# Taking the sums of squares for a norm inside the previous layer's output projection, in a two-layer streaming encoder

## The chip, the cores and the metric

One core of a Trainium2 chip runs the whole program. The metric is the device time of one execution in microseconds (us). The engines are named as the profile names them: PE does the matmuls, with PEld for its weight loads; DVE, ACT and POOL are the vector, scalar and general-purpose engines; SP only issues DMA transfers. Each engine works through its own list of instructions in order and waits at an instruction until the semaphores that it needs have come.

## The reference

Two layers run over a prompt of 2048 tokens and a sample of 64 new tokens, with a model width of 1024 and 16 heads of 64. Layer A is grouped-query attention over a sliding window, layer B attention over a band of chunks. Both have this form, in float32:

```python
def rms_norm(x, g):
    xf = x.astype(jnp.float32)
    y = xf * lax.rsqrt(jnp.mean(xf * xf, axis=-1, keepdims=True) + EPS)
    return (y * g.astype(jnp.float32)).astype(x.dtype)

def project(x, norm_g, w_in, q_g, k_g, n_heads, n_kv):
    h = rms_norm(x, norm_g)
    p = h @ w_in
    ...
    q, k, v, gate = jnp.split(p, [wq, wq + wkv, wq + 2 * wkv], axis=-1)
    ...
    return q, k, v, gate

def gated_attention_layer(...):
    qp, kp, vp, gp = project(x_p, norm_g, w_in, q_g, k_g, n_heads, n_kv)
    op = prompt_band_attention(qp, kp, vp, past_chunks, bias_fn, sinks)
    y_p = x_p + (op * jax.nn.silu(gp)) @ w_out
    ...
```

Layer B's input is layer A's output. Its norm needs one number per token: the mean of the squares of the token's 1024 values.

## The kernel before

**Data.** Activations lie in SBUF transposed, with the model's width on the 128 partitions (8 groups of 128) and the tokens along the free axis. The weights carry the norm's gain, and the per-token factor 1/rms is applied after the matmul, as the scale with which a projection leaves PSUM (`scaled`, L480, and `evacuate`, L488). So a projection may start before its tokens' factors are known; its evacuation may not. Every float32 operand of a projection is split into a high and a low part, and each product is three matmuls (L471, L472, L473; in the output projection L1269, L1270, L1271).

**Stages.** First comes layer A's input projection and attention, then layer A's output projection (668.7 to 873.8 us in the trace), then layer B's eight passes, one per pair of heads, and layer B's output projection. Between layers, x lies in HBM (`x1`). The stages overlap: projections and output projections are generators in the class `Filler` (L601), and the attention pipelines pull matmuls out of it in the gaps of their own work. The order on PE is written by hand in this way. The order on DVE, ACT, POOL and SP is set by the framework's scheduler, and some jobs go through a queue of background work (`bg`, L228).

**Layer A's output projection** (`output_jobs`, L1237) has two halves, each of 512 output columns. Each half has 8 jobs, one per block of 264 tokens (OT). A job has four groups (m = 0 to 3) of 24 matmuls, each group into one of the two PSUM buffers called pj. For every second group the residual is loaded into a tile `res` (two buffers, L1264); DVE adds the PSUM group to it (L1274), and after every second group the sum is stored to `x1` (L1276). The next job's input comes into `xraw` (tag of three buffers), ACT casts it (L376) and POOL subtracts (L377).

**Layer B's first pass** (`add_unit`, L979) takes units of 256 tokens, as two tiles of 128; the sample's 64 tokens are a unit of their own, next to last. `load_act` (L342) loads `x1` in four pieces per unit, casts (L376), subtracts (L377), and stores the split pieces for the seven later passes (L380). With `squares` set, which is so in the first pass only, each piece is also squared by ACT (L388) into a `res` tile, the two halves of that are added by DVE (L392), and the four pieces' sums are added up (L394). `token_scales` (L414) then sums over the partitions with a matmul by `ones` (L421) for each tile of tokens, adds eps on DVE (L424), and raises to the power of -0.5 on POOL (L428). It is called between the unit's first tile and its second (L1005, L1006) and puts its result into a pj buffer, the tag from which the projections' PSUM comes too. The sums over all 16 tiles of the prompt and the sample's tile are taken in nine such calls.

**Other names.** `BT` (L177) is a tile of 1920 columns that holds the attention biases; L189 loads it from `skew`. L556 makes the low part of the probabilities (`pl`), L583 is a PE transpose, L1174 and L1175 are layer B's probability-times-V matmuls, L1100 subtracts the row maximum, L306 makes the low part of weights, L917 is layer A's probability-times-V matmul, and L558 splits the cached keys and values of the sample (`KSA`, `KSB`, `VS`), which come through a `res` tile as well.

Of the kernel before, what the change touches and what calls it, by code (L numbers as in the profile page):

```python
# [11 lines left out]
AF = mybir.ActivationFunctionType  # L12
ALU = mybir.AluOpType
# [38 lines left out]
def hybrid_encoder_kernel(  # L52
# [360 lines left out]

    def token_scales(layer, unit, x, ps):  # L414
        for q, q2 in zip(x.items, x.squares):
            bg.run(q)
            bg.run(q2)
        part = x.sum[0]
        _, T, tiles = unit
        for i, (tt, t0, n) in enumerate(tiles):  # L420
            nc.tensor.matmul(ps[:, 2 * i : 2 * i + 2], part[:, i * P : (i + 1) * P], ones, start=True, stop=True)  # L421
        v = t("ms", [P, 4])
        w = len(tiles)
        nc.vector.tensor_scalar(  # L424
            v[:, : 2 * w], ps[:, : 2 * w], 1.0 / D, EPS, op0=ALU.mult, op1=ALU.add
        )
        tt = tiles[0][0]
        nc.gpsimd.tensor_tensor(  # L428
            rr[layer][:, tt : tt + w],
            v[:, : 2 * w].rearrange("p (i e) -> p i e", e=2)[:, :, 0],  # L430
            mhalf[:, :w],
            op=ALU.pow,
        )

    def row_scales(unit):
        _, T, tiles = unit
        w = len(tiles)
        tt = tiles[0][0]
        acc = t("ms", [P, 4])
        for i, (_, t0, n) in enumerate(tiles):  # L440
            r0 = (tt + i) * P
            for h in range(2):
# [6 lines left out]
                )  # L449
        v = t("ms", [P, 4])  # L450
        av = acc[:, : 2 * w].rearrange("p (i e) -> p i e", e=2)
# [195 lines left out]
    def layer_a():  # L647
# [4 lines left out]
        def add_unit(qd, place, unit):  # L652
# [58 lines left out]
            def first():  # L711
# [7 lines left out]
                for i, c in enumerate(both([project(it.tile, xc, st.w[qd], 512, o) for it, o in zip(mine, qgs)])):  # L719
                    if i == 7:  # L720
                        token_scales(0, unit, xc, psum("tp", 512, 1))
                        for it, o in zip(mine, kvs):
                            take_kv(it, o[0])
                    yield c
                for it, o in zip(mine, qgs):
                    take_qg(it, o[0])
                st.bias[0] = spread_first()
                token_scales(0, units[1], st.x[0, 1], psum("o", 512, 1))
                yield 2 * 3 * 512 / 2400
# [197 lines left out]
        def pipeline():  # L927
            N = len(items)
            for i in range(-3, N + 1):
# [5 lines left out]
                if 0 <= i < N:  # L935
                    scores(items[i])
                    bg.share(AL, AP_)
                filler.to(c0 + 0.3 * (end - c0))
# [35 lines left out]
    def layer_b():  # L974
# [4 lines left out]
        def add_unit(hp, unit):  # L979
# [7 lines left out]
            def prefetch():  # L987
                for j in range(NO):
                    assert finished["x1", j] == 2 or j * OT >= u * UT + T
                st.x[hp, u] = x = load_act(x1, u * UT, T, hp == 0, T == TS, None, xs[1], hp > 0)  # L990
                return x
# [6 lines left out]
            def gen():  # L998
# [3 lines left out]
                for e, (tt, t0, n) in enumerate(tiles):  # L1002
                    out = []
                    c = yield from project((tt, t0, n), xc, st.w[hp], 512, out)
                    if hp == 0 and e == 0:  # L1005
                        token_scales(1, unit, xc, psum("pj", 512, 2))  # L1006
                    pr = evacuate(1, tt, n, out[0], 512, P, it.gate[:, e])
                    it.prs.append(pr)
                    v, kn = pr[:n, 256:384], pr[:n, 128:256]
                    split_v(n, v, VS[:, 2] if last else VT[:, tt])  # L1010
                    it.todo += head_norm(n, pr[:n, 0:256]) + gate(n, it.gate[:n, e])
                    if last:
                        it.todo.append(store_kv(1, n, kn, v, kb_s[192:256, cols], vb_s[192:256, cols]))
# [221 lines left out]


    def output_jobs(layer, half, xin, xout):  # L1237
        st = Item()
# [7 lines left out]
        def add_unit(j):  # L1246
# [9 lines left out]
            def gen():  # L1256
                oc = st.x.pop(j)
                w = st.w
                for m in range(4):
# [15 lines left out]
                    if m % 2:  # L1275
                        store(xout[:, c : c + 2, o : o + OT], rv)  # L1276
                    if m == 3:
                        key = ("x1", "y")[layer], j
                        finished[key] = finished.get(key, 0) + 1
# [131 lines left out]
```

## Time and profile before

| what | value |
|---|---|
| time, three runs | median 2330.56 us (2327.19 to 2331.63) |
| the profiled execution's own time | 2335.05 us |
| its span, first to last instruction | 2333.3 us |
| mean granted PE clock | 0.994 |
| layer A's output projection | 668.7 to 873.8 us |
| layer B's first pass | 875.65 to about 1035 us |

The span is the part of the profiled execution's time between its first and last instruction; 1.75 us lie around it. "Idle before <- X" in a line means that the engine had nothing to do until X had finished. PEclk is the granted clock of PE as a share of full speed. In a timeline, a row marked x4 stands for four instructions like it that follow each other, and its duration is theirs together.

### The profile page before, as it was taken

How to read it: one execution, taken by the hardware profiler on the slowest of the kernel's cores; microseconds unless marked ns; L12 is line 12 of the kernel's file. 1: busy time of each engine (PE TensorE's matmuls, PEld its weight loads, DVE VectorE, ACT ScalarE, POOL GpSimd, SP SyncE). 2: the span in 40 equal slices, each digit the busy share in tenths (PEclk: the TensorE clock that was granted, in tenths of full speed). 3: DMA queues.
4: the chain of work that ended last, by engine and by line, in shares of the span. 5: the costliest groups of instructions: out<-in, count | busy, mean ns of one | idle time of the engine just before them, and what ended most of it. 6: DMA issues, size and time to landing. Idle time of an engine off the chain costs nothing.

```text
span 2333.3 us, 42430 instructions
## 1 busy us (share of the span) xinstructions
PE 2275.2 (98%) x13981; PEld 1990.6 (85%) x13981; DVE 1546.6 (66%) x5220; ACT 1435.4 (62%) x3644; POOL 844.0 (36%) x1187
## 2 busy tenths in 40 slices
PE   8999999999999999999999999999999999999999
PEld 6787788888889997878888888888888888888999
DVE  6778788888782227876766767767667677676211
ACT  6778677777773226765665656656656666566321
POOL 5554433333355446532222222222222222224443
PEclk9999999999999999999999999999999999999999
DMA  8746656545346676454444543544445435443665
GB/s 260 239 149 213 201 174 204 179 142 166 107 139 192 213 214 240 144 182 142 140 153 123 155 141 105 178 134 139 145 132 154 141 101 178 132 125 106 187 186 148
DMA packets 232125, 379.37 MB, mean 163 GB/s; under 512 B 24720, under 2 KB 163360, under 8 KB 231872
## 3 DMA queue, kind: packets, MB, share of 16 engines
q1 hardware_dynamic: 231904, 376.65, 52.3%
q8 instruction: 110, 1.80, 0.3%
q14 instruction: 111, 0.91, 0.1%
HBM read 296.13 MB, written 82.08 MB: 162 GB/s over the span
## 4 chain that ended last, share of the span: by engine, by line
PE 75%; DVE 9%; DMA 8%; ACT 5%; issue 2%; POOL 1%; SPq 0%; POOLq 0%; ACTq 0%; DVEq 0%
PE pj L471 12%; PE pj L473 12%; PE pj L472 12%; PE sb L583 5%; PE pj L1269 5%; PE pj L1270 5%; PE pj L1271 4%; PE o L1175 3%; PE o L1174 3%; PE tp L583 3%; PE sb L1096 3%; PE sb L1097 2%; PE sa L583 2%; DMA xraw<-in_x_rows_dram 1%; DVE sq L510 1%
## 5 line engine op out<-in xcount | busy, mean ns | idle before, releaser
L471 PE MATMUL pj<-wh,xx 128*128 128x512 f32 (+1 forms) x1648 | 670.2, 407 | 20.3 <-DVE ms L424 6.3
L473 PE MATMUL pj<-wh,xx 128*128 128x512 f32 (+1 forms) x1648 | 640.1, 388 | 0.0
L472 PE MATMUL pj<-wl,xx 128*128 128x512 f32 (+1 forms) x1648 | 637.1, 387 | 0.5 <-DVE wl L306 0.5
L473 PEld LDWEIGHTS pj<-wh,xx 128*128 128x128 f32 x1648 | 311.3, 189 | 67.2
L471 PEld LDWEIGHTS pj<-wh,xx 128*128 128x128 f32 x1648 | 312.5, 190 | 62.9 <-ACT pb L483 5.5
L377 POOL TENSOR_TENSOR xx<-xraw,xx 128x528 fp32r<-128x528 f32 (+1 forms) x200 | 265.1, 1342 | 229.8 <-ACT xx L376 225.0
L472 PEld LDWEIGHTS pj<-wl,xx 128*128 128x128 f32 x1648 | 313.2, 190 | 40.3 <-DVE wl L306 2.5
L514 POOL TENSOR_TENSOR f<-f,mhalf 128x4 f32<-128x4 f32 (+3 forms) x221 | 228.6, 1034 | 228.2 <-DVE f L510 221.1
L1104 ACT ACTIVATE p<-p,nm 128x640 f32<-128x640 f32 (+5 forms) x272 | 204.4, 751 | 157.5 <-DVE nm L1100 155.4
L1269 PE MATMUL pj<-xx,wh 128*128 128x264 f32 x1024 | 293.4, 287 | 1.0 <-DVE res L1274 1.0
L1270 PE MATMUL pj<-xx,wh 128*128 128x264 f32 x1024 | 291.3, 284 | 0.0
L1271 PE MATMUL pj<-xx,wl 128*128 128x264 f32 x1024 | 289.8, 283 | 0.0
L556 DVE TENSOR_TENSOR pl<-sb,ph 128x640 fp32r<-128x640 f32 (+5 forms) x288 | 196.9, 684 | 123.8 <-ACT ph L555 121.3
L1100 DVE CUSTOM_DVE_ANT_0 p<-sb,BT 128x640 f32<-128x640 f32 (+5 forms) x272 | 196.6, 723 | 118.4 <-PE sb L1097 114.9
L376 ACT CAST xx<-xraw 128x528 fp32r<-128x528 f32 (+1 forms) x200 | 123.5, 626 | 227.0 <-PE pj L1271 126.5
L555 ACT CAST ph<-sb 128x640 fp32r<-128x640 f32 (+5 forms) x288 | 167.2, 581 | 120.9 <-PE sb L583 113.2
L970 POOL TENSOR_TENSOR o<-gt,o 128x256 f32<-128x256 f32 (+2 forms) x140 | 107.2, 766 | 368.3 <-issue 158.8
L1274 DVE TENSOR_TENSOR res<-pj,res 128x264 f32<-128x264 f32 x128 | 55.0, 431 | 248.4 <-PE pj L1271 228.9
L1269 PEld LDWEIGHTS pj<-xx,wh 128*128 128x128 f32 x1024 | 192.7, 188 | 1.7 <-DVE res L1274 1.2
L1270 PEld LDWEIGHTS pj<-xx,wh 128*128 128x128 f32 x1024 | 192.4, 188 | 0.2
L1271 PEld LDWEIGHTS pj<-xx,wl 128*128 128x128 f32 x1024 | 192.6, 188 | 0.0
L583 PEld LDWEIGHTS sb<-ident,p 128*128 128x128 f32 (+2 forms) x1168 | 139.5, 140 | 52.1 <-issue 11.3
(186 smaller groups left out, 4840.9 us busy)
## 6 DMA issues: line engine op xcount, KB each, us to landing
xx<-xsb SPq DMA_DIRECT2D x224, 512.0 KB, 4.3
xx<-xsa SPq DMA_DIRECT2D x88, 512.0 KB, 4.6
xraw<-oga SPq DMA_DIRECT2D x64, 264.0 KB, 3.4
xraw<-ogb SPq DMA_DIRECT2D x64, 264.0 KB, 3.2
xsa<-xx SPq DMA_DIRECT2D x32, 512.0 KB, 4.6
wraw<-in_w_in_b_dram SPq DMA_DIRECT2D x64, 256.0 KB, 3.5
xsb<-xx SPq DMA_DIRECT2D x32, 512.0 KB, 3.9
xraw<-in_x_dram SPq DMA_DIRECT2D x40, 256.0 KB, 4.1
```

The costliest lines, as they stand in the source:

```text
L377: nc.gpsimd.tensor_tensor(xl, rv, xh.bitcast(F32), op=ALU.subtract)
L471: nc.tensor.matmul(ps[:n, :C], xh, wh, start=k == 0, stop=False)
L472: nc.tensor.matmul(ps[:n, :C], xh, wl, start=False, stop=False)
L473: nc.tensor.matmul(ps[:n, :C], xl, wh, start=False, stop=k == KC - 1)
L514: nc.gpsimd.tensor_tensor(fv, fv, mhalf[:n, :H], op=ALU.pow)
L556: b = nc.vector.tensor_tensor(dst_lo, src, dst_hi.bitcast(F32), op=ALU.subtract)
L583: nc.tensor.transpose(out, in_, ident[:n, :n])
L1100: mi = nc.vector.tensor_tensor_reduce(out=p[:n, :nk], in0=S[:n, o : o + nk], in1=bias[:n, b0 : b0 + nk], op0=ALU.add, op1=ALU.min, scale=1 ...
L1104: ex = nc.scalar.activation(p[:n, :nk], p[:n, :nk], AF.Exp, scale=-1.0, bias=nmh, accum_out=it.sm[:n, 2 * i + h : 2 * i + h + 1],)
L1269: nc.tensor.matmul(ps[:, :OT], wh, oh, start=k == 0, stop=False)
L1270: nc.tensor.matmul(ps[:, :OT], wh, ol, start=False, stop=False)
L1271: nc.tensor.matmul(ps[:, :OT], wl, oh, start=False, stop=k == KC - 1)
```

## The change

With the change, layer B's first pass squares nothing: `load_act` is called with `squares` false for every unit of layer B, and the call of `token_scales` between the two tiles is gone. Instead, each time a job of layer A's output projection has stored two groups (32 times), `sum_squares` squares the two on ACT (528 columns, L1254 of the changed kernel) into a tile `p`, one of three, and DVE adds the two halves into a running sum over all the model's width (L1258, L1260; 70 adds in all where there were 63). These sums lie in the columns of `BT`, which no bias uses by then; the last 192 tokens lie in a tile `row`. In the second half, when a block's columns are complete, `block_scales` does the matmuls by `ones` (L425 of the changed kernel) into the PSUM tag `o`, the addition of eps (L427) and the power, after group m = 1 of the next job; for the last block and the sample it does so in layer B's first unit, after the evacuation of the first tile. The number of matmuls by `ones` stays.

In the changed kernel the lines after L414 are numbered differently: L471, L472 and L473 become L473, L474 and L475, L1274 becomes L1306, and L424 becomes L427.

```diff
+    def sums_to_scales(layer, tt, parts, ps):
+        w = len(parts)
+        for i, part in enumerate(parts):
+            nc.tensor.matmul(ps[:, 2 * i : 2 * i + 2], part, ones, start=True, stop=True)
...
-                st.x[hp, u] = x = load_act(x1, u * UT, T, hp == 0, T == TS, None, xs[1], hp > 0)
+                st.x[hp, u] = x = load_act(x1, u * UT, T, False, T == TS, None, xs[1], hp > 0)
...
-                    if hp == 0 and e == 0:
-                        token_scales(1, unit, xc, psum("pj", 512, 2))
                     pr = evacuate(1, tt, n, out[0], 512, P, it.gate[:, e])
...
+                    if it is its[0] and e == 0:
+                        block_scales(TOK - OT)
...
+    cut = 15 * P
+
+    def sums(a, b):
+        if "sums" not in held:
+            held["sums"] = t("row", [P, VL], 2)
+        assert b <= 6 * P or "scored" in held
+        if b <= cut:
+            c = (a + 4 * P) % cut
+            return BT[:, c : c + b - a]
+        return held["sums"][:, a - cut : b - cut]
+
+    def sum_squares(first, o, rv):
+        s2 = t("p", [P, 640], 3)[:, : 2 * OT].rearrange("p (k s) -> p k s", k=2)
+        nc.scalar.activation(s2, rv, AF.Square)
+        ends = sorted({o, o + OT} | {x for x in (cut - 4 * P, cut) if o < x < o + OT})
+        for a, b in zip(ends, ends[1:]):
+            dst, x = sums(a, b), s2[:, :, a - o : b - o]
+            nc.vector.tensor_tensor(dst, x[:, 0] if first else dst, x[:, 1], op=ALU.add)
+            if not first:
+                nc.vector.tensor_tensor(dst, dst, x[:, 0], op=ALU.add)
+
+    def block_scales(o):
+        tiles = [tt for tt in range(NT) if o < (tt + 1) * P <= o + OT]
+        if o + OT == TOK:
+            nc.vector.tensor_copy(sums(TOK, TOK + TS), sums(SEQ, TOK))
+            tiles.append(NT)
+        sums_to_scales(1, tiles[0], [sums(tt * P, (tt + 1) * P) for tt in tiles], psum("o", 512, 1))
...
                     if m % 2:
                         store(xout[:, c : c + 2, o : o + OT], rv)
+                        if layer == 0:
+                            sum_squares(half == 0 and m == 1, o, rv)
+                            if half and m == 1 and j:
+                                block_scales(o - OT)
```

**Where instructions move.** The first place is PE in layer B's first pass, at the last unit (tokens 1792 to 2047), between its two tiles of 128 tokens. `pj` with its numbers is a PSUM buffer in use, `sqr` the unit's sum of squares. Before:

```order
L471 MATMUL pj_13131<-wh_11392,xx_13097 128x512
L472 MATMUL pj_13131<-wl_11393,xx_13097 128x512
L473 MATMUL pj_13131<-wh_11392,xx_13097 128x512
L421 MATMUL pj_13261<-ones,sqr_13061 128x2 x2
L471 MATMUL pj_13272<-wh_11051,xx_13055 128x512
L472 MATMUL pj_13272<-wl_11052,xx_13055 128x512
L473 MATMUL pj_13272<-wh_11051,xx_13055 128x512
```

And with the change:

```order
L473 MATMUL pj_13097<-wh_11518,xx_13059 128x512
L474 MATMUL pj_13097<-wl_11519,xx_13059 128x512
L475 MATMUL pj_13097<-wh_11518,xx_13059 128x512
L473 MATMUL pj_13232<-wh_11178,xx_13045 128x512
L474 MATMUL pj_13232<-wl_11179,xx_13045 128x512
L475 MATMUL pj_13232<-wh_11178,xx_13045 128x512
L585 MATMUL sb_13238<-ident,p_13175 128x128 x5
```

The matmuls by `ones` have left this place, and the second tile's projection follows the first's at once; the same holds for the other units.

The second place is DVE in the second half of layer A's output projection, over two jobs. `res` is a residual tile, `pj` a PSUM group. Before there are only the four additions of each job:

```order
L1274 TENSOR_TENSOR res_10952<-pj_10954,res_10952 128x264
L1274 TENSOR_TENSOR res_10952<-pj_10980,res_10952 128x264
L1274 TENSOR_TENSOR res_11019<-pj_11021,res_11019 128x264
L1274 TENSOR_TENSOR res_11019<-pj_11085,res_11019 128x264
L1274 TENSOR_TENSOR res_11118<-pj_11120,res_11118 128x264
L1274 TENSOR_TENSOR res_11118<-pj_11146,res_11118 128x264
```

And with the change (`p` holds the squares, `o` the sums over the partitions):

```order
L427 TENSOR_SCALAR ms_10928<-o_10925 128x4
L1258 TENSOR_TENSOR BT<-BT,p_10921 128x264
L1260 TENSOR_TENSOR BT<-BT,p_10921 128x264
L1306 TENSOR_TENSOR res_10931<-pj_10933,res_10931 128x264
L1306 TENSOR_TENSOR res_10931<-pj_10959,res_10931 128x264
L1258 TENSOR_TENSOR BT<-BT,p_10986 128x264
L1260 TENSOR_TENSOR BT<-BT,p_10986 128x264
L1306 TENSOR_TENSOR res_10996<-pj_10998,res_10996 128x264
L1306 TENSOR_TENSOR res_10996<-pj_11038,res_10996 128x264
L427 TENSOR_SCALAR ms_11072<-o_11069 128x4
```

After every second L1306 two additions into `BT` have come in, and once per job an L427; the four L1306 of a job keep their order.

The third place is DVE at the join of layer A's last output job and layer B's first unit. Before:

```order
L1274 TENSOR_TENSOR res_11309<-pj_11374,res_11309 128x264
L392 TENSOR_TENSOR sqr_11355<-res_11353 128x256
L394 TENSOR_TENSOR sqr_11324<-sqr_11324,sqr_11355 128x256
L392 TENSOR_TENSOR sqr_11371<-res_11369 128x256
L394 TENSOR_TENSOR sqr_11324<-sqr_11324,sqr_11371 128x256
L306 SCALAR_TENSOR_TENSOR wl_11379<-wraw_11073,gain,wh_11378 128x512
L306 SCALAR_TENSOR_TENSOR wl_11386<-wraw_11083,gain,wh_11385 128x512
L1274 TENSOR_TENSOR res_11413<-pj_11415,res_11413 128x264
L1274 TENSOR_TENSOR res_11413<-pj_11441,res_11413 128x264
L306 SCALAR_TENSOR_TENSOR wl_11393<-wraw_11093,gain,wh_11392 128x512
L392 TENSOR_TENSOR sqr_11488<-res_11486 128x256
L392 TENSOR_TENSOR sqr_11504<-res_11502 128x256
```

And with the change:

```order
L306 SCALAR_TENSOR_TENSOR wl_11512<-wraw_11210,gain,wh_11511 128x512
L1306 TENSOR_TENSOR res_11565<-pj_11593,res_11565 128x264
L306 SCALAR_TENSOR_TENSOR wl_11519<-wraw_11220,gain,wh_11518 128x512
L1258 TENSOR_TENSOR BT<-BT,p_11620 128x72
L1258 TENSOR_TENSOR row_9106<-row_9106,p_11620 128x192
L558 TENSOR_TENSOR KSA<-res_11947,KSA 64x256
L1260 TENSOR_TENSOR BT<-BT,p_11620 128x72
L1260 TENSOR_TENSOR row_9106<-row_9106,p_11620 128x192
L558 TENSOR_TENSOR KSB<-res_11947,KSB 64x256
L558 TENSOR_TENSOR VS<-res_11947,VS 128x2x64 x2
L1265 COPY row_9106<-row_9106 128x64
L427 TENSOR_SCALAR ms_11686<-o_11682 128x6
```

The additions of the first units' squares are gone. In their place stand the last block's, and between these, ahead of the copy L1265 and of L427, the four splits L558 of the cached keys and values, which wait for their load into `res_11947`.

On SP the loads of layer B's first biases (L189), for which BT must be free again, come later than before, each behind a matmul by `ones` that reads the columns they overwrite.

More of the change, by code (lines that the diff above doesn't have):

```diff
@@ L412, in hybrid_encoder_kernel, with token_scales @@
     rr = [const([P, NT + 1], f"rms{l}") for l in range(2)]
-    def token_scales(layer, unit, x, ps):
+    def token_scales(unit, x, ps):
         for q, q2 in zip(x.items, x.squares):
@@ L419, in token_scales @@
         _, T, tiles = unit
[L420 to L423, printed above, removed]
+        sums_to_scales(0, tiles[0][0], [part[:, i * P : (i + 1) * P] for i in range(len(tiles))], ps)
+    def sums_to_scales(layer, tt, parts, ps):
+        w = len(parts)
+        for i, part in enumerate(parts):
+            nc.tensor.matmul(ps[:, 2 * i : 2 * i + 2], part, ones, start=True, stop=True)
+        v = t("ms", [P, 8])
         nc.vector.tensor_scalar(
@@ L426, in token_scales @@
         )
-        tt = tiles[0][0]
         nc.gpsimd.tensor_tensor(
@@ L438, in row_scales @@
         tt = tiles[0][0]
-        acc = t("ms", [P, 4])
+        acc = t("ms", [P, 8])
         for i, (_, t0, n) in enumerate(tiles):
@@ L449, in row_scales @@
                 )
-        v = t("ms", [P, 4])
+        v = t("ms", [P, 8])
         av = acc[:, : 2 * w].rearrange("p (i e) -> p i e", e=2)
@@ L720, in first @@
                     if i == 7:
-                        token_scales(0, unit, xc, psum("tp", 512, 1))
+                        token_scales(unit, xc, psum("tp", 512, 1))
                         for it, o in zip(mine, kvs):
@@ L727, in first @@
                 st.bias[0] = spread_first()
-                token_scales(0, units[1], st.x[0, 1], psum("o", 512, 1))
+                token_scales(units[1], st.x[0, 1], psum("o", 512, 1))
                 yield 2 * 3 * 512 / 2400
@@ L936, in pipeline @@
                     scores(items[i])
+                    if i == N - 1:
+                        held["scored"] = True
                     bg.share(AL, AP_)
```

## The prediction

> **What bounds the kernel now.** I read the page first, then the waits of PE, then PE's and DVE's timelines at the longest of them. The page's span, its first line on engines and the chain that ended last:
>
> ```profile
> span 2333.3 us, 42430 instructions
> PE 2275.2 (98%) x13981; PEld 1990.6 (85%) x13981; DVE 1546.6 (66%) x5220; ACT 1435.4 (62%) x3644; POOL 844.0 (36%) x1187
> PE 75%; DVE 9%; DMA 8%; ACT 5%; issue 2%; POOL 1%; SPq 0%; POOLq 0%; ACTq 0%; DVEq 0%
> ```
>
> PE is busy for 98% of the span. The change leaves the number and the order of its projections as they were and moves the small matmuls by `ones`. So it can gain only where PE is idle or slowed around the moved work, and lose only where it makes PE idle anew. All the idle time of PE from the end of layer A's attention to the end of layer B's first pass, by what ended it (total us, times, longest):
>
> ```profile
> PE pj L471 <- DVE ms L424: 6.3, 6, 3.6
> PE pj L471 <- DVE res L1274: 1.9, 1, 1.9
> PE sb L583 <- DVE pl L556: 1.5, 1, 1.5
> PE o L1175 <- DVE pl L556: 1.4, 2, 1.0
> PE o L917 <- DVE pl L556: 1.3, 1, 1.3
> PE sb L583 <- DVE nm L1100: 1.2, 3, 0.8
> PE pj L1269 <- DVE res L1274: 1.0, 1, 1.0
> PE sb L583 <- ACT sq L527: 0.7, 1, 0.7
> PE tp L583 <- ACT gt L959: 0.2, 1, 0.2
> ```
>
> The first line is the wait of the second tile's projection for the norm's scales. The second is at the join of the layers. L917 is layer A's attention, and L1269 is the output projection. The five others belong to layer B's attention in its first pass: 1.5 + 1.4 + 1.2 + 0.7 + 0.2 = 5.0 us. The same table for 1030 to 2200 us, the passes that square nothing:
>
> ```profile
> PE sb L583 <- DVE nm L1100: 3.7, 7, 0.6
> PE tp L583 <- DVE KB L1057: 1.9, 2, 1.4
> PE tp L583 <- ACT gt L959: 1.2, 2, 0.9
> PE o L1175 <- DVE pl L556: 1.2, 5, 0.2
> ```
>
> That is 8.0 us in 1170, or 1.0 in 150, against 5.0 in the 150 of the first pass. Next, PE at the join and at the longest wait (start, duration, in brackets the idle time before):
>
> ```profile
> 875.65 0.47 PE L471 MATMUL pj<-wh,xx 128*128 128x512 f32 x1 [1.86 <-DVE res L1274]
> 880.07 0.39 PE L471 MATMUL pj<-wh,xx 128*128 128x512 f32 x1
> 882.81 0.50 PE L421 MATMUL pj<-ones,sqr 128*128 128x2 f32 x4
> 884.06 0.47 PE L471 MATMUL pj<-wh,xx 128*128 128x512 f32 x1 [0.75 <-DVE ms L424]
> 1019.91 0.80 PE L471 MATMUL pj<-wh,xx 128*128 128x512 f32 x1 [3.62 <-DVE ms L424]
> ```
>
> And windows of the trace: busy us of PE, PEld, DVE, ACT and POOL (with instructions), then the granted clock, the DMA share and GB/s:
>
> ```profile
> 800.00:850.00 50.00, 50.00 (x414) 50.00 (x413) 7.36 (x17) 11.58 (x19) 21.84 (x17) 1.00 0.66 194
> 875.00:1025.00 150.00, 138.02 (x746) 115.94 (x747) 120.34 (x369) 104.03 (x251) 80.78 (x93) 0.98 0.57 193
> 877.00:878.00 1.00, 1.00 (x4) 0.81 (x3) 1.00 (x1) 0.00 (x0) 0.93 (x1) 0.50 1.11 408
> 1020.00:1023.00 3.00, 3.00 (x11) 2.61 (x12) 0.83 (x2) 2.75 (x7) 1.80 (x4) 0.50 0.21 63
> ```
>
> In the output projection's second half DVE has 43 of 50 us free and ACT 38. In the first pass DVE is busy 120 of 150. The work moves from the crowded stage to the empty one. The last two rows show a second cost: after both long gaps PE runs at half clock.
>
> **The six waits for L424: -6.3.** Between a unit's two tiles, L421 takes one of the two pj buffers, and the second tile's first L471 waits until L424 has read it. With the change L421 isn't there (PE's order shows it), and the other buffer was left by the unit before. The whole 6.3 goes, unless something else is late at the same place. That matters at 1019.91 above all, and DVE's list just before shows what:
>
> ```profile
> 1007.45 1.38 DVE L392 TENSOR_TENSOR sqr<-res 128x256 f32<-128x256 f32 x1
> 1008.87 0.42 DVE L394 TENSOR_TENSOR sqr<-sqr,sqr 128x256 f32<-128x256 f32 x1
> 1012.94 0.41 DVE L392 TENSOR_TENSOR sqr<-res 128x256 f32<-128x256 f32 x1
> 1014.70 0.43 DVE L394 TENSOR_TENSOR sqr<-sqr,sqr 128x256 f32<-128x256 f32 x1
> 1018.22 0.82 DVE L556 TENSOR_TENSOR pl<-sb,ph 128x640 fp32r<-128x640 f32 x1
> 1019.70 0.16 DVE L424 TENSOR_SCALAR ms<-pj 128x4 f32<-128x4 f32 x1
> ```
>
> Without the wait PE starts its three projection matmuls at about 1016.3 (1019.91 - 3.62) and reaches L1175, which needs L556's `pl`, some 1.4 us later (0.7 for the three, 0.5 for the five transposes behind them, 0.2 for L1174), at 1017.7. In before `pl` is ready at 1019.04. The four additions of squares ahead of it took 1.38 + 0.42 + 0.41 + 0.43 = 2.64 us and are gone. If all of that reaches `pl`, it is there at 16.4 and nothing waits; if none does, 1.3 comes back. I take half of the relief (17.7, just in time) and put **+0.4** for what is left.
>
> **The join: -1.9.** DVE's last two residual additions there, with the square's addition behind them, and SP's wait that made the residual late:
>
> ```profile
> 875.07 0.77 DVE L1274 TENSOR_TENSOR res<-pj,res 128x264 f32<-128x264 f32 x2 [1.20 <-DMA res<-in_x_dram]
> 876.72 1.49 DVE L392 TENSOR_TENSOR sqr<-res 128x256 f32<-128x256 f32 x1
> SPq L1264 <- DVE sqr L392: 1.3, 1, 1.3
> ```
>
> The first pass's squares take `res` tiles, of which there are two, while the last output job still needs one for its residual. So the residual's load started late, the addition too, and layer B's first projection waited 1.86 us for the PSUM buffer. With the change no square takes a `res` tile, and the load can start a group earlier. The load of the cached keys, which now comes before, takes one only after the last residual has its own.
>
> **The half clock: -1.7 and -1.6.** After the gap at the join, the first tile took from 875.65 to 882.81, 7.16 us for its 24 matmuls. The last 12 of them, from 880.07 on, took 2.74, so 24 at full speed take 5.5, and 1.7 was lost. The second gap is followed by a stretch that is at half clock through 1020 to 1023, which loses half of its 3 us and a little: 1.6. Both go if their gaps go. [...]
>
> **Attention in the first pass: -2.5.** The first pass loses the squares' work, by these groups:
>
> ```profile
> L392 DVE TENSOR_TENSOR sqr<-res x44: 214/426/1510, 5.6 to 1012.9; 128x256 f32<-128x256 f32 x40, 128x64 f32<-128x64 f32 x4
> L388 ACT ACTIVATE res<-xraw x44: 307/628/650, 5.0 to 1010.2; 128x512 f32<-128x512 f32 x40, 128x128 f32<-128x128 f32 x4
> ```
>
> Some 36 of each lie in layer B: 36 x 0.63 = 23 us of ACT, and for DVE 36 additions between 0.43 and 1.5 with some 27 L394 of 0.42, 27 to 65 us, of 120. The waits on DVE and ACT in between, 5.0 us, can go wholly (-5.0), fall to the rate of the later passes (-4.0), or stay (0). The casts, subtractions and stores of the split pieces stay in this pass and not in the later ones, so I take the middle, -2.5.
>
> **What is added in layer A's output projection: +0.3 and +0.3.** 50 us hold 414 matmuls, so a group of 24 takes 2.9 us and a job 11.6. Let a job's clock start with its first matmul. L1306 of m = 3 ends at about 12.2, the square (0.63) at 12.9, and two additions at 0.43, with handovers, at 13.9. DVE's next need is the next job's m = 0, whose matmuls end at 14.6, and PE needs that buffer only when m = 2 starts, at 17.5. So the additions may end 17.5 - 0.5 - 13.9 = 3.1 us later before PE waits; after m = 1 it is much the same. The cover is DVE's idle time. Without it each group would cost up to 0.9. L425, with up to three weight loads, was paid before, too. L427 in the idle DVE costs nothing; its PSUM tag `o` is idle by then. In the first half DVE still ends layer A's attention: at most another wait like L917's 1.3, and I take 0.3. At the join of the halves ACT and DVE split new weights, where the 1.0 of L1269 may grow, to 2.7 at the most if the two additions (0.9) and the square (0.63) fall into it whole, or go; again 0.3. SP's delayed bias loads have nothing behind them that is needed within their wait, so 0.
>
> **The last block: +0.5.** Its L425 stands on PE right behind layer B's first tile, at 11.6 + 5.5 = 17.1 on the last job's clock. DVE reaches the copy ahead of it only after the four L558, and these wait for a load. The rows are a load of the keys (KB, us to landing), SP's wait from 860 to 1030 us, and a store of `x1`:
>
> ```profile
> res<-in_ckt_b_dram SPq DMA_DIRECT2D x8, 128.0 KB, 4.4
> SPq L380 <- POOL xx L377: 72.4, 26, 8.3
> x<-res SPq DMA_DIRECT2D x3, 264.0 KB, 3.4
> ```
>
> The `res` tile for it comes free when the store after m = 1 has landed, at about 9.7 (6.3 and 3.4 us for a store), and the keys are there at 14.1. The splits, additions and copy still to come are some six of 0.43: 16.7, in time by 0.4. But SP issues the load, and if it stands behind one of the waits of L380 (72.4 / 26 = 2.8 us) all moves to 19.5 or so, 2.5 late. So the bounds are 0 and 2.5, or 4.2 with a half-clock stretch of 1.7 behind it. I take 0.5, near the order's own margin.
>
> **The sum.** 2335.05 - 6.3 + 0.4 - 1.9 - 1.7 - 1.6 - 2.5 + 0.3 + 0.3 + 0.5 = 2322.55, which is 12.5 below the profiled execution's time. That lies 4.5 above the median of the three runs (2330.56), so I set the same 12.5 against the median: **2318.1**.
>
> **Rivals.**
> *DVE is still late (0.14).* The waits of L424 at 1005 and 1019 (about 1.0 of the 2.7 that isn't the longest, and 3.6) become waits for `pl`, the half clock stays (1.6), and so do attention's 2.5. For it: DVE has no idle row from 1005 to 1019. Against it: 2.64 us of squares stood right before `pl`. It gives 2318.1 + 1.0 + 3.6 + 1.6 + 2.5 - 0.4 = 2326.4.
> *The last block's sums come late (0.10).* PE stands 2.5 us at L425 and runs at half clock behind it: 2318.1 - 0.5 + 4.2 = 2321.8.
> *All of attention's waits go (0.10),* and nothing is late anew: 2318.1 - 2.5 - 1.1 = 2314.5.
> *Slower: the additions are blocked (0.06).* L392 took 1.49 at 876.72, and POOL was then in a run of L377. If both additions of each group meet such a run, they end 2 x (1.49 - 0.43) = 2.1 us later, inside the 3.1. From 1.0 us of lateness of the square in ACT's queue on, PE stalls, and behind a run of casts as here it would be 2.1:
>
> ```profile
> 860.03 2.08 ACT L376 CAST xx<-xraw 128x528 fp32r<-128x528 f32 x3 [3.73 <-PE pj L1271]
> ```
>
> Then each of 16 jobs loses 4.2 - 3.1 = 1.1 us, 17.6 in all: 2335.7. Against it stands the idle DVE, which seldom meets POOL twice. [...]
> That the change doesn't do what it says is excluded: PE's order shows L421 gone from between the tiles.
>
> **Numbers.** The forecast has the remaining 0.60. The range is 2312.5 to 2326.5: below, all of attention's waits and the spread of the runs; above, the rival with a late DVE. A measurement can tell 0.2%, or 4.7 us. Faster by more (below 2325.9): 0.60 + 0.10 + 0.10 and a little of the late DVE, 0.82; within it, the rest of that rival, 0.12; slower, 0.06.
>
> **What would show it.** Right: no wait between the two tiles of a unit, no gap and clock 1.00 at the join, attention's waits in the first pass near 2.5, none in the output projection beyond 1.0. A wait at L425 on PE shows the second rival, waits for `pl` near the end of the first pass the first, waits of L1269 in every job for L1306 the slower one. The prediction is wrong as a whole if PE's idle time in 660 to 1030 us falls by less than 5 us, or if it falls and the time doesn't.

## The result, and the profile after

The changed kernel took 2311.64 us (median of 4 runs, 2308.83 to 2314.97) against 2330.8 for the kernel before (4 runs). The ratio is 0.9929, with a 95% interval of 0.9914 to 0.9944: 16.5 us less, with 13 to 20 us inside the interval (the two medians of four stand 19.2 us apart). A second measurement, with 5 runs of the one and 27 of the other, gave 0.9926 (0.9912 to 0.9940), 17.3 us. The forecast was 12.5 less; the direction is right and the size is some 4 to 5 us short. As a time, 2311.64 lies 0.9 us below the stated range (2312.5 to 2326.5); by the ratio, against the 2330.56 from which the forecast was counted, it would be 2314.0, inside it. The profiled execution took 2308.83, its page begins:

```profile
span 2307.1 us, 42442 instructions
PE 2266.7 (98%) x13981; PEld 1986.4 (86%) x13981; DVE 1562.2 (68%) x5226; ACT 1439.4 (62%) x3640; POOL 844.6 (37%) x1186
PE 79%; DVE 7%; DMA 6%; ACT 5%; issue 2%; POOL 1%; SPq 0%; POOLq 0%; ACTq 0%; DVEq 0%
```

PE holds 79% of the chain that ended last, where it held 75%; the shares of DVE and DMA fell. The waits of PE over the output projection and the first pass, 600 to 1030 us:

```profile
PE pj L1301 <- DVE res L1306: 1.3, 2, 0.8
PE o L919 <- DVE pl L558: 1.2, 1, 1.2
PE sb L585 <- DVE pl L558: 1.2, 1, 1.2
PE sb L1100 <- ACT pa L485: 0.7, 1, 0.7
PE tp L585 <- DVE KB L1061: 0.5, 1, 0.5
PE sb L585 <- ACT sq L529: 0.4, 1, 0.4
PE sb L1100 <- DVE nm L1104: 0.2, 1, 0.2
```

The line for the norm's scales is gone, and so is the one at the join. Layer B's attention waits 1.2 + 0.7 + 0.5 + 0.4 + 0.2 = 3.0. The table of before had 5.0 for it, but that table ends at 1030 us, 28 us before the end of its first pass (1057.6 us by the windows below, not about 1035); another 0.5 for KB follows there, so like for like it is 5.5 against 3.0. PE around the last block's sums, in layer B's first unit:

```profile
871.64 0.40 PE L475 MATMUL pj<-wh,xx 128*128 128x512 f32 x1
871.88 0.28 PE L425 MATMUL o<-ones,BT 128*128 128x2 f32 x2
872.02 0.87 PE L425 MATMUL o<-ones,row 128*128 128x2 f32 x4
872.75 0.48 PE L473 MATMUL pj<-wh,xx 128*128 128x512 f32 x1
```

L425 starts right behind the first tile; the splits of the cached keys ahead of its additions were in time but for 0.2 us, a wait for the copy L1265 behind them. The two stages stand below as windows (busy us of PE, PEld, DVE, ACT, POOL; granted clock; DMA), the output projection up to layer B's first matmul, and the first pass from there to the first sample matmul on `VS`. For the changed kernel:

```profile
657.60:866.36 208.76, 206.18 (x1677) 203.66 (x1676) 108.30 (x235) 91.22 (x183) 101.69 (x100) 1.00 0.65 194
866.36:1031.60 165.24, 162.17 (x909) 136.79 (x907) 118.51 (x382) 110.55 (x273) 82.82 (x100) 1.00 0.62 208
```

And for the kernel before:

```profile
668.70:875.65 206.95, 202.87 (x1648) 200.40 (x1648) 70.54 (x170) 75.96 (x158) 96.69 (x92) 1.00 0.65 197
875.65:1057.60 181.95, 170.16 (x935) 142.89 (x935) 141.48 (x442) 122.91 (x301) 89.22 (x106) 0.98 0.55 187
```

The first pass fell by 16.7 us. 8.7 of it is idle time of PE (11.8 to 3.1), the rest is busy time: two stretches at half clock, the matmuls by `ones` that moved out, and a remainder of 1.3 us that is taken up further below. The output projection grew by 1.8: PE is busy 3.3 us longer there with those matmuls (206.18 against 202.87) and idle 1.5 less, the join's wait being gone and small ones come. Together the two stages are 14.9 us shorter, and everything after them takes the same (1275.7 us before and 1275.5 now to the end of the span). The 11 us by which the start of layer A's output projection differs between these two executions (668.7 and 657.6 us) is not the change's: no instruction is moved there, and eleven further profiles, of both programs and of variants, put it anywhere from 659.5 to 669.9.

### The profile page after: what moved, and what is told of

The parts are those of the page before. It is cut to its first block, busy times and chain, and to the rows that moved or that the text cites. A ratio compares the mean times of both kernels' runs of the same rounds, so it can differ in the third digit from the quotient of the medians.

```text
span 2307.1 us, 42442 instructions
## 1 busy us (share of the span) xinstructions
PE 2266.7 (98%) x13981; PEld 1986.4 (86%) x13981; DVE 1562.2 (68%) x5226; ACT 1439.4 (62%) x3640; POOL 844.6 (37%) x1186
## 4 chain that ended last, share of the span: by engine, by line
PE 79%; DVE 7%; DMA 6%; ACT 5%; issue 2%; POOL 1%; SPq 0%; POOLq 0%; ACTq 0%; DVEq 0%
PE pj L473 13%; PE pj L475 12%; PE pj L474 12%; PE pj L1301 5%; PE sb L585 5%; PE pj L1302 5%; PE pj L1303 5%; PE o L1179 3%; PE o L1178 3%; PE sb L1100 3%; PE sb L1101 3%; PE tp L585 3%; PE sa L585 2%; DMA xraw<-in_x_rows_dram 1%; DMA row<-vec 1%
## 5 line engine op out<-in xcount | busy, mean ns | idle before, releaser
L473 PE MATMUL pj<-wh,xx 128*128 128x512 f32 (+1 forms) x1648 | 668.9, 406 | 9.9 <-DVE pb L488 3.9
L475 PE MATMUL pj<-wh,xx 128*128 128x512 f32 (+1 forms) x1648 | 639.2, 388 | 0.0
L474 PE MATMUL pj<-wl,xx 128*128 128x512 f32 (+1 forms) x1648 | 636.0, 386 | 1.4 <-DVE wl L306 1.4
L475 PEld LDWEIGHTS pj<-wh,xx 128*128 128x128 f32 x1648 | 310.8, 189 | 67.0
L473 PEld LDWEIGHTS pj<-wh,xx 128*128 128x128 f32 x1648 | 312.4, 190 | 51.0 <-ACT wh L303 4.1
L474 PEld LDWEIGHTS pj<-wl,xx 128*128 128x128 f32 x1648 | 312.9, 190 | 40.9 <-DVE wl L306 3.1
L377 POOL TENSOR_TENSOR xx<-xraw,xx 128x528 fp32r<-128x528 f32 (+1 forms) x200 | 265.7, 1345 | 203.6 <-ACT xx L376 191.2
L558 DVE TENSOR_TENSOR pl<-sb,ph 128x640 fp32r<-128x640 f32 (+5 forms) x288 | 197.0, 684 | 126.2 <-ACT ph L557 123.8
L557 ACT CAST ph<-sb 128x640 fp32r<-128x640 f32 (+5 forms) x288 | 167.3, 581 | 126.5 <-PE sb L585 118.5
L376 ACT CAST xx<-xraw 128x528 fp32r<-128x528 f32 (+1 forms) x200 | 122.3, 626 | 185.4 <-PE pj L1303 98.7
L1306 DVE TENSOR_TENSOR res<-pj,res 128x264 f32<-128x264 f32 x128 | 55.0, 430 | 200.7 <-PE pj L1303 197.6
L512 DVE CUSTOM_DVE_ANT_0 sq<-pa 128x64 f32<-128x64 f32 (+1 forms) x850 | 170.4, 253 | 23.3 <-ACT pa L485 21.3
```

The source lines that it names most:

```text
L377: nc.gpsimd.tensor_tensor(xl, rv, xh.bitcast(F32), op=ALU.subtract)
L473: nc.tensor.matmul(ps[:n, :C], xh, wh, start=k == 0, stop=False)
L474: nc.tensor.matmul(ps[:n, :C], xh, wl, start=False, stop=False)
L475: nc.tensor.matmul(ps[:n, :C], xl, wh, start=False, stop=k == KC - 1)
L558: b = nc.vector.tensor_tensor(dst_lo, src, dst_hi.bitcast(F32), op=ALU.subtract)
```

## The experiments

**The two kernels again.** Unchanged, for the scatter.

> The kernel before, unchanged, to see how far one execution's stages scatter. In the two profiles shown so far the stretch ahead of layer A's output projection, in which no instruction was moved, took 668.7 us before and 657.6 after. If that 11 us is scatter, this profile may show anything from 655 to 672 there; if the changed program's memory layout makes layer A faster, it shows 668 to 670 again. In both cases the output projection up to layer B's first matmul takes 207 us, the first pass from there to the first sample matmul L1174 on VS 182 us, and the rest of the attention 1118 us, each within 1.5 us. Ratio 1.000.

> The changed kernel, unchanged. My terms give 12.5 us less than before (ratio 0.9946), the first measurement gave 0.9929. If layer A's 11 us was scatter, its stretch ahead of the output projection lies between 655 and 672 us in this profile and the ratio comes out at 0.993 to 0.995; if it belongs to the changed program, the stretch is 656 to 659 again and the ratio 0.990 to 0.993. The output projection takes 208.8 us, the first pass 165.2, the rest 1117.6, each within 1.5 us, in both cases.

Before came out at 1.0003 (0.9994 to 1.0012). Its layer A took 664.7 us up to the output projection, and the two stages 206.2 and 183.3. The changed kernel's took 660.9, then 207.9 and 164.7. So the two stages give 388.9 and 389.5 us for the one and 374.0 and 372.6 for the other, 15 to 17 us apart, which is the whole of the measured 16.5 to 17.3. Layer A scatters by some 10 us from one execution to the next, so the experiments below are judged by their ratio to before and by the sum of the two stages (373.3 for the changed kernel, 389.2 for before, the means of two profiles each; a stage sum comes from a single execution). Where a loss against the changed kernel is given by the ratio, it is against a ratio of 0.9927, between the two that were measured for that kernel, and by the intervals it is good to some 4 us.

The join looks different in this second profile of before:

```profile
870.91 0.47 PE L471 MATMUL pj<-wh,xx 128*128 128x512 f32 x1 [2.33 <-ACT xx L376]
```

The gap is about as long, but what ends it is ACT's cast of layer B's first input (L376, 870.27 to 870.87). DVE's last residual additions (L1274) started at 870.33, so two late causes stand side by side here. And no half clock follows this gap (the windows of 1 us from 871 to 879 show 1.00): a stretch of half clock comes only behind a wait of 1.70 us for L424, at 878.71.

**The squares put back, without their matmul.**

```diff
-                st.x[hp, u] = x = load_act(x1, u * UT, T, False, T == TS, None, xs[1], hp > 0)
+                st.x[hp, u] = x = load_act(x1, u * UT, T, hp == 0 and True, T == TS, None, xs[1], hp > 0)
...
+                    if hp == 0 and e == 0:
+                        for q, q2 in zip(xc.items, xc.squares):
+                            bg.run(q)
+                            bg.run(q2)
```

> The changed kernel, with the first pass's squares (ACT and DVE, in res tiles) done again as before, their sums unused; no matmul by ones waits for them. My theory, by which the waits for L424 and the crowded queue are separate terms: the join's residual wait and its half clock come back (1.9 + 1.7) and half of attention's waits (2.0 to 2.5), so the first pass takes about 171 us instead of 165, and the kernel about 6 us more than the changed one. The rival that the queue is everything: PE waits for pl and for evacuations at 1005 and 1019 instead of for L424, the first pass takes 177 to 179, 12 to 14 us more. The rival that only the wait on PSUM counted: 165 to 166, no difference to the changed kernel.

It took 2332.05 us, 1.0003 of before (0.9994 to 1.0011): the whole gain is gone, though no PE instruction waits for a norm's scales in this kernel. The lines of a variant have numbers of their own: L585 is again the transpose, L558 makes `pl`. Its longest PE waits:

```profile
PE sb L585 <- DVE pl L558: 3.9, 2, 2.7
PE pj L473 <- DVE res L1310: 3.5, 1, 3.5
PE o L1183 <- DVE pl L558: 2.2, 1, 2.2
PE sb L585 <- DVE nm L1108: 1.8, 2, 1.4
```

And its first pass as a window:

```profile
874.41:1051.50 177.09, 167.92 (x906) 140.34 (x906) 143.94 (x439) 123.54 (x300) 80.17 (x98) 0.97 0.58 191
```

The first pass takes 177.1 us, as the rival of the crowded queue had it (177 to 179), not 171. The stall that was a wait for L424 at the last unit is a wait for `pl` of 2.7 us at the transposes (L585) three matmuls further on in the program. The join's wait for a residual is back too, at 3.5 us. My theory of separate terms falls here.

**The PSUM buffer alone, in the kernel before.**

```diff
-                        token_scales(1, unit, xc, psum("pj", 512, 2))
+                        token_scales(1, unit, xc, psum("tp", 512, 1))
```

> The kernel before, with only one thing changed: the matmul by ones of layer B's first pass writes into the PSUM tag tp instead of pj, so that the second tile need not wait until L424 has read. Squares, res tiles and the place of the matmul stay. If the wait for the PSUM buffer is a term of its own: the six waits for L424 (6.3) and the half clock after the longest (1.6) go, 6 to 8 us less than before (ratio 0.9966 to 0.9974), the first pass 174 to 176 us. If the crowded DVE list is the cause, waits for pl and pb take their place: 0 to 3 us less.

No gain: 1.0005 (0.9996 to 1.0014). Two of its lines:

```profile
PE tp L583 <- DVE ms L424: 6.7, 6, 1.7
PE pj L471 <- DVE res L1274: 3.1, 1, 3.1
```

The projection no longer waits, but the queries' transposes (L583), which share `tp`, wait for the same L424: six times again and 6.7 us in all (6.3 and 7.2 in before's profiles), though no longer than 1.7 at once. In this profile half clock took 6.8 us, against 3.4 in before's. The wait was handed on, not removed, so this run alone does not separate the theories. The next puts the wait back without the squares.

**The wait alone, without the squares.**

```diff
+                    if hp == 0 and e == 0:
+                        sums_to_scales(1, tiles[0][0], [ident] * len(tiles), psum("pj", 512, 2))
...
-                    if it is its[0] and e == 0:
-                        block_scales(TOK - OT)
...
-                            if half and m == 1 and j:
-                                block_scales(o - OT)
```

> The changed kernel, its sums still taken in layer A's output projection, but the matmuls by ones, the eps and the power done where the kernel before had them: in the first pass, between the two tiles of each unit, through a pj buffer. (They read a constant tile in place of the sums, so layer B's norm is left out.) Only the wait on PSUM is put back, without the squares' load. If the wait is a term of its own, as my sum had it, some 6 us of waits for L427 return and the kernel takes 6 to 8 us more than the changed one. If the waits were the crowded queue seen at one place, they shrink to the bare way from PE to DVE and back, 0.2 to 0.4 for each unit, and the kernel takes 1 to 3 us more.

Its ratio is 0.9968 (0.9956 to 0.9981), 9.6 us more than the changed kernel, and 7.9 more by the two stages (381.2). Its longest waits:

```profile
PE pj L473 <- DVE ms L427: 4.9, 3, 2.9
PE sb L585 <- DVE nm L1104: 2.6, 2, 1.4
```

The first pass as a window:

```profile
870.69:1046.90 176.21, 167.06 (x936) 141.59 (x935) 120.04 (x391) 109.86 (x272) 86.83 (x108) 0.99 0.58 196
```

So the wait costs something without the squares as well, about as much as I had given it (6.3 and 1.6). The rival that it would shrink to 1 to 3 us falls. DVE is busy only 120 of 176 us in this pass, and the wait still reaches 2.9. DVE's list at the longest of them shows why:

```profile
1009.78 0.81 DVE L1104 CUSTOM_DVE_ANT_0 p<-sb,BT 128x640 f32<-128x640 f32 x1
1010.52 0.08 DVE L1104 DVE_READ_ACCUMULATOR2_ANT nm<- 128x1 f32 x1
1010.52 0.15 DVE L427 TENSOR_SCALAR ms<-pj 128x4 f32<-128x4 f32 x1
```

L427 takes 0.15 us, but it stands behind a run of the attention's own work on DVE that has no idle row from 1003.3 us on. So even here it is a queue that PE waits for, one without squares in it. The variant also makes the evacuations of the first tile wait for the scales again; of that the profile shows 0.2 us in all (ACT L487 for POOL's power L430).

**The squares' two halves, each alone.** DVE's additions on a constant tile, and ACT's squares into small tiles:

```diff
+        def dead(c):
+            def fn():
+                part = t("sqr", [P, 2 * T if joint else T], 2)
...
+                nc.vector.tensor_tensor(w, d, d, op=ALU.add)
+                if x.sum:
+                    nc.vector.tensor_tensor(x.sum[0][:, :T], x.sum[0][:, :T], part[:, :T], op=ALU.add)
...
+            elif src is x1 and cache is not None:
+                x.squares.append(bg.put(0.7, dead(c)))
...
```

```diff
+        def dead(c):
+            def fn():
+                s2 = t("sqr", [P, 256], 2).bitcast(mybir.dt.bfloat16)[:, : 2 * T].rearrange("p (k s) -> p k s", k=2)
+                nc.scalar.activation(s2, raws[c], AF.Square)
+            return fn
...
+            elif src is x1 and cache is not None:
+                x.squares.append(bg.put(0.7, dead(c)))
...
```

> The changed kernel with the DVE half of the first pass's squares alone put back: the same number of additions of 256 columns, on a constant tile, their result unused; no square on ACT, no res tile, no later load. With all of the squares back the kernel lost 16 to 18 us against the changed one, about 12 in the first pass and 4 at the join. If DVE's list is what makes PE wait, this one loses 6 to 12 us, in waits for pl and nm. If ACT's squares, the res tiles or the later loads count, it loses 0 to 3.

> The changed kernel with the ACT half of the first pass's squares alone put back (into small tiles of their own, of 16 bits, unused): no addition on DVE, no res tile; xraw is held until the square has read it, as before. If ACT's list is what makes PE wait, it loses 6 to 12 us against the changed kernel; if DVE's list or the res tiles count, 0 to 3. My guess is that DVE (busy 120 of 150 us in the first pass) counts for more than ACT (104 of 150).

DVE's half alone gives 0.9968 (0.9956 to 0.9981), 9.6 us more than the changed kernel by the ratio and by the stages of its profile; ACT's alone 0.9956 (0.9942 to 0.9969), 6.8 more by the ratio and 3.8 by the stages. The longest waits with DVE's half back (L600 is the transpose, L573 makes `pl`):

```profile
PE tp L600 <- ACT gt L978: 3.8, 4, 1.4
PE sb L600 <- DVE pl L573: 3.4, 2, 2.3
```

Its first pass:

```profile
870.84:1043.80 172.96, 164.62 (x909) 137.62 (x907) 139.38 (x424) 109.72 (x273) 82.96 (x100) 0.99 0.60 199
```

The longest waits with ACT's half back (L593 the transpose, L566 for `pl`):

```profile
PE sb L593 <- DVE pl L566: 3.7, 2, 2.3
PE tp L593 <- ACT gt L971: 0.7, 3, 0.3
```

Its first pass:

```profile
878.00:1047.00 169.00, 162.78 (x909) 136.80 (x907) 115.03 (x383) 124.92 (x305) 82.43 (x100) 1.00 0.61 203
```

The profiles point to DVE's list as the one that counts for more, as guessed, but the two intervals overlap, so that the order isn't shown. ACT's half also ends in waits for `pl`. The instruction that makes `pl` needs ACT's copy of the high part: on the changed kernel's page DVE is idle for 126.2 us before L558, and ACT's L557 ended 123.8 of that. So a late ACT can make a late DVE. The 3.8 us of waits for ACT's gate (L978) with DVE's half back I had not expected; why they come is open.

**The squares back for all but the first two units.**

```diff
-                st.x[hp, u] = x = load_act(x1, u * UT, T, False, T == TS, None, xs[1], hp > 0)
+                st.x[hp, u] = x = load_act(x1, u * UT, T, hp == 0 and u > 1, T == TS, None, xs[1], hp > 0)
...
```

> The changed kernel with the first pass's squares put back (ACT, DVE and res tiles, unused) for all units but the first two, which are the ones that meet layer A's last output jobs. If the join's residual wait with its half clock is a term of its own, this kernel keeps the join's 4 to 5 us, and loses only the first pass's 10 to 12 us against the changed kernel. If the first pass waits only because it starts late from the join, it loses 0 to 4.

The join stays clean: the output projection takes 208.5 us and no L473 waits for a residual. Still the ratio is 0.9997 (0.9985 to 1.0009), 16 us lost; in its profile, the fastest of 11 executions, the two stages take 13.5 more. So the first pass loses nearly everything by itself, and the join isn't its cause. The first pass as a window:

```profile
868.03:1046.30 178.27, 167.02 (x909) 138.91 (x907) 143.81 (x432) 122.34 (x301) 83.25 (x100) 0.98 0.58 193
```

**The join alone, in the kernel before.**

```diff
-                s2 = t("res", [P, 2 * OT], 2)[:, : 2 * T].rearrange("p (k s) -> p k s", k=2)
+                if src is x1 and o < 2 * UT:
+                    s2 = t("p", [P, 640], 3)[:, : 2 * T].rearrange("p (k s) -> p k s", k=2)
+                else:
+                    s2 = t("res", [P, 2 * OT], 2)[:, : 2 * T].rearrange("p (k s) -> p k s", k=2)
```

> The kernel before, with one change: the squares of layer B's first two units go into tiles p instead of res, so that the last output jobs' residual loads find a free res tile. If the residual's wait at the join is a term of its own, it goes with its half clock (1.9 to 2.3 and 1.7), the stretch from the output projection's start to layer B's first matmul falls from 206 to 207 us to 204 to 205, and the kernel takes 3 to 4 us less than before (ratio 0.9985). If something else is late at the join (a cast, the split of the weights), it gains 0 to 1.

The ratio is 0.9993 (0.9983 to 1.0003), 1.6 us less, no gain that can be told from none. Two of its waits:

```profile
PE pj L474 <- DVE ms L427: 6.5, 6, 3.6
PE tp L586 <- DVE pa L522: 1.5, 1, 1.5
```

And its two stages:

```profile
660.50:865.24 204.74, 203.12 (x1649) 200.58 (x1648) 69.74 (x168) 72.66 (x153) 94.62 (x90) 1.00 0.66 197
865.24:1048.40 183.16, 168.80 (x936) 141.94 (x934) 143.60 (x444) 124.99 (x305) 91.20 (x107) 0.99 0.56 188
```

The join's wait is gone and the output projection takes 204.7, as expected. The half clock behind the join is gone too (the first pass has one such stretch, at 1011 to 1015). But the first pass isn't shorter than before's 182.0 and 183.3: a new wait of 1.5 for L522 stands at 885 us, and waits for `nm` (L1103) come to 2.1 where before had 1.2 and 1.8. As I read it, PE came earlier to work that DVE did no earlier.

**What the moved work costs where it is now.** No sums at all, and twice the sums:

```diff
+    nc.gpsimd.memset(rr[1], 0.5)
...
-                    if it is its[0] and e == 0:
-                        block_scales(TOK - OT)
...
-                            sum_squares(half == 0 and m == 1, o, rv)
-                            if half and m == 1 and j:
-                                block_scales(o - OT)
+                            pass
```

```diff
         nc.scalar.activation(s2, rv, AF.Square)
+        d2 = t("p", [P, 640], 3)[:, : 2 * OT].rearrange("p (k s) -> p k s", k=2)
+        nc.scalar.activation(d2, rv, AF.Square)
+        nc.vector.tensor_tensor(d2[:, 0], d2[:, 0], d2[:, 1], op=ALU.add)
+        nc.vector.tensor_tensor(d2[:, 0], d2[:, 0], d2[:, 1], op=ALU.add)
```

> The changed kernel with no sums of squares for layer B at all (its norm is left out, a constant stands for 1/rms): nothing in layer A's output projection, nothing in the first pass. It shows what the moved work still costs. If the squares and additions are covered by ACT's and DVE's idle time, only the matmuls by ones go, some 4.4 us on PE (34 of them, 0.5 us for four), and a residual addition's wait of 0.3: 4 to 5 us less than the changed kernel. If the additions delay the output projection, 7 us or more.

> The changed kernel with the squares and additions in layer A's output projection done twice (one more square on ACT and two more additions of 264 columns on DVE for each of the 32 groups, unused): some 20 us of ACT and 28 us of DVE more. By my slack of 3.1 us for each group nothing waits for it: 0 to 1 us more than the changed kernel, the output projection 208 to 210 us. If the additions are blocked beside POOL's subtractions and the slack is used up, each of the 16 jobs loses about 1 us or more, 16 us in all.

Without the sums the ratio is 0.9907 (0.9890 to 0.9925), 4.7 us less than the changed kernel's, and the two stages 368.3 us, 5.0 less. That is the matmuls by `ones`, as expected: PE's busy time in the two stages is 363.4 us here and 368.4 and 367.7 in the changed kernel's profiles. The squares and additions themselves are covered all but for about a microsecond. The output projection:

```profile
665.00:868.66 203.66, 202.43 (x1648) 200.33 (x1647) 67.31 (x162) 71.84 (x151) 94.70 (x91) 1.00 0.67 198
```

DVE has 108.3 - 67.3 = 41 us more to do there in the changed kernel, and PE's idle time in that stage is 2.6 and 2.1 us in the changed kernel's two profiles against 1.2 here. Twice the work gives 0.9957 (0.9944 to 0.9969), 7 us more (6.3 by the stages), where I expected 0 to 1. Most of it comes from one place, the start of the first half (PE's timeline, in brackets the idle time before):

```profile
696.98 0.39 PE L1305 MATMUL pj<-xx,wh 128*128 128x264 f32 x1 [3.11 <-DVE res L1310]
723.46 0.39 PE L1305 MATMUL pj<-xx,wh 128*128 128x264 f32 x1 [1.33 <-DVE res L1310]
```

A half-clock stretch behind the first loses 1.7 more. There DVE still has layer A's attention to finish. After 724 us no job waits, so the rival by which blocked additions stall every job fails even with twice the additions, and my slack was enough where DVE is free.

## Why the prediction was right in sign and short in size

- **The six waits for L424 (-6.3).** They are gone, as said. For what is late next at the last unit I had put 0.4; it is the wait of 1.2 for L558's `pl` in the table above (at 996.14 us, and at the transposes L585, not at the matmul that I had named). It is counted below among attention's waits.
- **The join (-1.9).** Gone in the changed kernel. Taken out alone it gave 1.6 us, which can't be told from nothing, where I had 1.9 + 1.7.
- **The half clock (-1.7 and -1.6).** Both stretches are gone: summed over windows of 1 us, the clock lost 3.4 us in before and 0 in the changed kernel. Before's second profile has two stretches as well, but there none belongs to the join's gap. That I tied one to the join was right for the one execution that I had.
- **Attention in the first pass (-2.5).** Over the whole pass the listed waits fell by 2.5, from 5.5 to 3.0. The middle between nothing and all was a choice, 2.5 us from either end, so the exact hit is luck.
- **What is added (+0.3, +0.3, +0.5).** L1306 makes PE wait 1.3 instead of 1.0, L919 as before L917; L425 waited 0.2. Some +0.5 in all. The blocked additions of the slower rival did come. I had said that DVE seldom meets POOL; from 790 to 850 us one group's first addition in each job, five in all, falls into a run of three L377 on POOL and takes 1.55 to 1.69 us, and the other group's takes 0.43 to 0.50. The slack took it in. One such job:

```profile
804.54 3.92 POOL L377 TENSOR_TENSOR xx<-xraw,xx 128x528 fp32r<-128x528 f32 x3 [3.25 <-issue]
807.10 1.65 DVE L1258 TENSOR_TENSOR BT<-BT,p 128x264 f32<-128x264 f32 x1 [0.76 <-ACT p L1254]
812.95 0.43 DVE L1258 TENSOR_TENSOR BT<-BT,p 128x264 f32<-128x264 f32 x1 [0.62 <-ACT p L1254]
```

- **The sum.** By the waits and clock of the two profiles it is -6.3 - 1.9 - 3.4 - 2.5 + 0.5 = -13.6, 1.1 from the forecast's 12.5. The two stages fell by 14.9, and by 16.9 in the second pair. Two things make up the rest. PE's busy time, without half clock and with the matmuls by `ones` balanced, fell by another 1.3 to 1.5 us, which the list of waits does not show; what it comes from, no run shows. And before's own waits scatter: in its second profile L424 made 7.2 us, the join 2.3, and L1100 1.8.

The total was near, but a step of the prediction failed all the same: the attribution. The prediction gave some 8 us to the wait for the scales and its half clock, 3.6 to the join, and 2.5 to the squares' load on ACT and DVE, and added them. The runs show that these are not terms to be added:

| put back into the changed kernel | us lost by the ratio |
|---|---|
| the wait alone | 9.6 |
| DVE's additions alone | 9.6 |
| ACT's squares alone | 6.8 |
| all squares, not at the join | 16 |
| all squares, with the join, no wait | 17.7 |
| everything (the kernel before) | 16.5 to 17.3 |

Each is worth 7 to 10 alone, and all together 17. With some 4 us to each row, the rows are too close to be put in order, but their sum is clear: the wait alone and all squares without it lose 9.6 + 17.7 = 27.3, and everything together 16.5 to 17.3. As I read it, one chain in the first pass runs from PE through ACT and DVE back to PE, and whichever of them is late makes the one stall at each unit; the squares alone are enough to fill it. On the changed kernel's page, over the whole span, PE's L585 ended 118.5 us of ACT's idle time before L557, as L557 ended 123.8 of DVE's before L558. The sum came near because the change removes everything at once. As forecasts of a single part, the same terms failed twice: the PSUM buffer alone was given 6 to 8 us and the join alone 3 to 4, and neither gained anything that can be told from none. My rival "DVE is still late" had the mechanism right (a wait for L424 turns into one for `pl`), but it needs the squares still in the queue, and the change takes them out. What is left between the changed kernel and the one without sums, 5 us, is nearly all PE's own time for the matmuls by `ones` (4.3 to 5.0 us of busy time).

## What to carry to other kernels

Idle time of an engine that stands in a loop with PE was not all slack here. DVE was busy for 118.5 of 165 us in the changed kernel's first pass (72%); additions that nobody waited for brought it to 139.4 of 173 (81%) and cost about 10 us, and with ACT's squares 16 to 18, where before's listed waits of attention came to 5. Here it paid to move such work to a stage in which the engine was at 34%: 41 us of DVE there cost PE about a microsecond of idle time. It did cost more where that stage's start was still full of the work before it, as the doubled sums show (gaps of 3.11 and 1.33 us on PE). And before pricing a wait by its line in the table, ask what is late next at that instant: a wait that has a second cause right behind it may be worth nothing until both are gone. Here the PSUM buffer alone came out at 1.0005 of before, and the join alone at 0.9993.

## What was not expected of the hardware

Over the two stages, by windows of 1 us, a stretch of half clock lost 1.70 or 1.71 us in every profile but one, and a profile had none, one, two or three of them. The exception is the profile with the PSUM buffer moved, in which one stretch from 871 to 878 us lost 3.41. The length of the gap alone didn't decide whether one followed. In the kernel with the wait alone, a gap of 1.62 us brought one and a gap of 2.89 did not. PE's timeline (start, duration, idle before):

```profile
878.40 0.50 PE L473 MATMUL pj<-wh,xx 128*128 128x512 f32 x1 [1.62 <-DVE ms L427]
1010.73 0.50 PE L473 MATMUL pj<-wh,xx 128*128 128x512 f32 x1 [2.89 <-DVE ms L427]
```

And windows of PE's busy time, clock, DMA share and GB/s, 3 us from shortly behind each:

```profile
879.00:882.00 3.00, 3.00 (x10) 0.58 1.00 368
1011.00:1014.00 3.00, 3.00 (x23) 1.00 0.09 25
```

Behind before's gap of 1.86 us at the join, the four windows from 876 to 880 us show clocks of 0.72, 0.50, 0.50 and 0.57. That is 1.71 us lost, and at a clock of 0.50 it makes a stretch of 3.42 us. Why the gap of 1.62 us was followed by such a stretch and the one of 2.89 was not, no run here shows.
